# A two-group hybrid layer on one core: late weights split in small pieces along the convolution stage, the second weight part used last, query and key columns set between others

## The chip, the cores and the metric

The kernel runs on one core of a Trainium2 chip. The metric is device time in microseconds, the median of three runs of the whole kernel. TensorE (PE in the profile) multiplies, VectorE (DVE), ScalarE (ACT) and GpSimd (POOL) do the elementwise work, and all DMA transfers are issued by SyncE (SP), whose queue works in order.

## What is computed

One trunk layer for 2048 latent tokens and 256 context tokens, 1024 channels wide:

```python
h = rmsnorm(x) * norm_g * (1 + scale) + shift
q, k, v, g_att, a_conv, g_conv, x_pool, g_pool, x_ssm, g_ssm, g_mrg = split(h @ w_in)   # 70 x 128 columns
o_att  = windowed attention with a sink; latent queries and keys rotated, they also see the context keys
o_conv = silu(layernorm(depthwise_conv31(a0 * sigmoid(a1))))
o_pool = (mean over windows 2, 4, 8, 16 - x_pool) @ w_pool * scale
o_ssm  = z0 * sigmoid(z1),  z = gelu(bidirectional_scan(x_ssm)) @ glu_w
proj   = [o_n * silu(g_n)] @ w_br[n]                    # four branches
y = rmsnorm(x + gate * (sum_n(sigmoid(g_mrg[n]) * proj[n]) @ w_out)) * final_g
```

Everything is float32. The kernel keeps this accuracy on TensorE by splitting each operand into a high part, rounded to the matrix format, and a low part, the rest; a product is then three matmuls: high by high, low activation by high weight, high activation by low weight.

## The kernel before, in words

The 2304 tokens are cut into six chunks of 384 columns, two chunks to a group, three groups (0, 1, 2); channels lie on partitions. Tiles `hh` and `hl` hold the two parts of a group's normalized input, 8 slices of 128 channels each. A *dense column* is 128 columns of `w_in` for one group: `dense` (line 588) calls `mm3` (414) for both chunks, 24 matmuls of 128x128 by 128x384 each, so 48 per column. Before, `mm3` walks over the 8 slices and does the three products of a slice after one another.

A weight tile is split when it is first used (`split`, 357: `hi` is an ACT copy, `lo` a DVE subtraction, names `wis`, `wih`, `wil`) and both parts are stored to DRAM; for later groups `fetch` (390) loads them. `weights` (397) asks for them two columns ahead.

The order of TensorE's work is written out by hand, with a planner. `flow` (202) runs one dense stream and a list of background streams; each is a generator that yields what it needs next. A small cost model (`Clock`, 41) says when that will be ready; the first background stream that is ready goes, otherwise the dense stream makes a step (half a slice pair or the like; 10 steps to a column). `self.steps` counts dense steps, and some background work is paced by it (`METER`). PE then executes exactly this order and waits wherever the real data are later than the model said. The other engines' orders are made by the framework's scheduler.

Stages: (0) modulation, normalized inputs and the state-space branch's projections (`xssm`, 604); (1) all 66 columns of group 2 and then some of group 1, with the state-space scan in the background; (2) the rest of group 1, group 0's value, query and key columns, then its other columns and the 32 merge columns of group 1 again; in the background the depthwise convolution (`conv_taps`, DVE, ACT and POOL; `conv_norm`), the pools (`pool_tile`) and, from the 1350th microsecond on, attention; (3) per group the gated linear unit (`glu_group`), the four branch projections (`merge_group`, name `pj`) and the output projection (`out_group`), with `last_norm` in the background.

Names in the profile: `mm` is the PSUM tile of dense columns, `mge` the merge gates' copies out of it, `qf` and `qs` a query or key column and its swapped halves, `plh` and `plp` a pool's split and its product, `lnh` and `mean` the same for the convolution's layer norm, `dg` and `rb` the diagonal and the broadcast of a norm, `gy` the inputs of the linear unit, `wps`, `wph`, `wpl` the pieces of the late weights (`glu_w`, `w_br`, `w_out`) in `presplit` (374), and `wd_...` split weights in DRAM. Before, `presplit` is called from `gates_late` (1811) during the last 28 merge columns of stage 2, after attention has ended, up to three weights to a column. All instructions carry line 162, the recording helper, so they are told apart by their tiles.

Of the kernel before, what the change touches and what calls it, by code (L numbers as in the profile page):

```python
# [21 lines left out]
CH = 384  # L22
# [165 lines left out]
class K:  # L188
    def __init__(self, tc, A, outs):
        self.tc, self.A, self.O = tc, A, outs  # L190
        self.clock = Clock()
        self.nc = ClockedCore(self.clock, tc.nc)
        self.wplan, self.wgot, self.wsplit, self.waits, self.half, self.norms = [], {}, {}, {}, {}, 0
        self.wcache, self.have, self.steps = {}, {}, 0
# [179 lines left out]
    def presplit(self, key, ap):  # L374

        kt = self.WSRC[key[0]][1]
        src = self.A[self.WSRC[key[0]][0]][key[1:] if len(key) > 2 else key[1]]
        d = self.dp.tile([2, 128, kt, 128], F32, name="wd_" + "_".join(str(x) for x in key))
        for k in range(0, kt, 4):
            st = ap.tile([128, 4, 128], F32, name="wps", tag="p", bufs=2)  # L380
            self.load(st, src[:, k:k + 4])
            h = ap.tile([128, 4, 128], F32R, name="wph", tag="ph", bufs=3)
            l = ap.tile([128, 4, 128], F32R, name="wpl", tag="pl", bufs=3)
            self.hi(h, st)
            self.lo(l, st, h)
            for i, x in enumerate((h, l)):
                self.store(d[i][:, k:k + 4], f32(x))
        self.wcache[key] = d
# [25 lines left out]
    def mm3(self, outs, w, xs, kt):  # L414

        nc = self.nc
        wh, wl = w
        for c, o in enumerate(outs):
            yield (wh, wl, o, *xs[c](0), *xs[c](min(1, kt - 1)))
            for k in range(kt):  # L420
                for p, (wt, part) in enumerate(((wh, 0), (wh, 1), (wl, 0))):
                    nc.tensor.matmul(o, wt[:, k, :], xs[c](k)[part], start=(k == 0 and p == 0),
                                     stop=(k == kt - 1 and p == 2))
                if k % 2 == 1 and k + 2 < kt:
                    yield (*xs[c](k + 1), *xs[c](k + 2))
                elif k % 2 == 1:
                    yield ()
# [158 lines left out]
    PAIRS = {5: 0, 36: 37, 68: 69}  # L586

    def dense(self, ct, hs):
        xs = [lambda k, h=h: (h[0][:, k, :], h[1][:, k, :]) for h in hs]
        if ct in self.half:  # L590
            w, ps = self.half.pop(ct)
        else:
            w, ps = self.weights(("in", ct)), []
        for c in range(len(ps), len(hs)):
            ps.append(self.pm())
            yield from self.mm3([ps[c]], w, [xs[c]], 8)
            if c == 0 and ct in self.PAIRS and self.PB["mm"] > 2:
                nt = self.PAIRS[ct]
                self.half[nt] = self.weights(("in", nt)), [self.pm()]
                yield from self.mm3(self.half[nt][1], self.half[nt][0], xs[:1], 8)  # L600
# [32 lines left out]
    def col_qk(self, g, j, hs):  # L633
# [11 lines left out]
        qf = self.evq.tile([128, GT], F32, name="qf", tag="ev", bufs=3)  # L645
# [4 lines left out]
        qs = self.evq.tile([128, GT], F32, name="qs", tag="ev", bufs=3)  # L650
# [5 lines left out]
        r = self.evq.tile([128, GT], F32, name="qr", tag="ev", bufs=3)  # L656
# [3 lines left out]
        h = self.evq.tile([128, GT], F32R, name="qh", tag="evr", bufs=2)  # L660
        l = self.evq.tile([128, GT], F32R, name="ql", tag="evr", bufs=2)
# [6 lines left out]
        self.store(dst[1, j], f32(l))  # L668

    def col_v(self, g, hs):  # L670
        nc = self.nc
        ps = yield from self.dense(5, hs)
        vf = self.evq.tile([128, GT], F32, name="vf", tag="ev", bufs=3)
# [6 lines left out]
    def v_tokens(self, g, vf):  # L680

        nc = self.nc
        h = self.evq.tile([128, GT], F32R, name="vh", tag="evr", bufs=2)
        l = self.evq.tile([128, GT], F32R, name="vl", tag="evr", bufs=2)

        def half(a):
            tp = self.px("vtp", "x")[:, :CH]
# [67 lines left out]
    def conv_setup(self, cp):  # L755
# [11 lines left out]
        self.pw = cp.tile([128, 4, 128], F32, name="pw")  # L767
        self.load(self.pw, A["pool_w"])
        self.pwh = cp.tile([128, 4, 128], F32R, name="pwh")
        self.pwl = cp.tile([128, 4, 128], F32R, name="pwl")  # L770
        self.hi(self.pwh, self.pw)
        self.lo(self.pwl, self.pw, self.pwh)
# [5 lines left out]
    def convolution(self, chunks, mp):  # L778
# [14 lines left out]
        def pools():  # L793
            for gc in chunks:
                yield (lambda gc=gc: self.there("px", gc, 8),)
                for i in range(4):
                    yield from self.pool_tile(gc, i, mp)
# [18 lines left out]
    def conv_taps(self, gc, mp, taps):  # L816
# [4 lines left out]
        def tap(i, t):  # L821
            if t == 0:
                bufs[i] = mp.tile([128, CH + 60], F32, name="cbuf", tag="cbuf", bufs=3)
                self.n0 = self.seg_load(bufs[i], self.cx_d[i], gc, 15, self.CP) - 30
                accs[i] = mp.tile([128, self.W], F32, name="acc", tag="acc", bufs=8)
# [14 lines left out]
        for k in range(31):  # L840
# [5 lines left out]
            yield accs[i], lambda n=taps[0]: self.steps >= n * self.METER  # L846
        return accs

    def conv_norm(self, gc, accs, mp):
# [3 lines left out]
        for i in range(4):  # L853
# [5 lines left out]
            yield h, l, mean  # L859
            nc.tensor.matmul(mean, self.o512, h[:, :N], start=(i == 0), stop=False)  # L860
# [26 lines left out]
    def pool_tile(self, gc, i, mp):  # L887
# [735 lines left out]
    def last_norm(self, g, y, S, mp, chunks):  # L1623
# [5 lines left out]
        yield S, st  # L1629
        Sf = S.rearrange("p c t -> p (c t)")  # L1630
        for i in range(n):
# [7 lines left out]
        for m, c in enumerate(chunks):  # L1639
# [4 lines left out]
            yield dg, rb  # L1644
            nc.tensor.matmul(rb[:, :CH], self.ones, dg.rearrange("p i q -> p (i q)"), start=True, stop=True)
# [7 lines left out]
    def run(self, upto=9):  # L1653
        tc, nc, A = self.tc, self.nc, self.A
        ctx = ExitStack()
        with ctx:
# [28 lines left out]
            with era:  # L1685
# [11 lines left out]
                def qkv(g):  # L1697
                    return [([5], lambda h: self.col_v(g, h))] + [([j], lambda h, j=j: self.col_qk(g, j, h))
                                                                  for j in range(5)]
# [255 lines left out]
```

## Time and profile before

| | us |
|---|---|
| median of three runs | 3170.85 (3159.23 to 3172.75) |
| profiled execution, its own time | 3164.44 |
| its span | 3162.5 |
| PE busy | 2949.8 |
| DVE busy | 2031.0 |
| ACT busy | 1035.6 |
| POOL busy | 872.3 |

Mean granted clock of TensorE: 0.968 of full speed. DMA moved 711.13 MB, 225 GB/s over the span. An engine's busy time is the time in which at least one of its instructions ran; what stands in square brackets behind an instruction is the idle time just before it and what ended it.

### The profile page before, as it was taken

To read this page: it belongs to the slowest core of one execution; us is meant where nothing else is said; L and a number is where in the kernel's file an instruction comes from. 1 tells how busy PE (TensorE), PEld (TensorE's weight loads), DVE (VectorE), ACT (ScalarE), POOL (GpSimd) and SP (SyncE) were. 2 spreads that over 40 slices of the span, in tenths; PEclk is the share of its full clock that TensorE was granted. 3 is DMA by queue.
4 is the path that set the end of the run, shared out by engine and by line. 5 is a ranking of instruction groups with operands and counts; after the bars stand their busy time and mean duration, and the time that the engine had idled before them with its cause. 6 is when DMAs were issued, how large, how long until landed. Compare 5 with 4: busy or idle time off the path is not lost.

```text
span 3162.5 us, 45875 instructions
## 1 busy us (share of the span) xinstructions
PE 2949.8 (93%) x16316; PEld 2820.6 (89%) x16316; DVE 2031.0 (64%) x3468; ACT 1035.6 (33%) x1972; POOL 872.3 (28%) x1124
## 2 busy tenths in 40 slices
PE   8988999999989997899999999998867999999998
PEld 4888999998889987899999999998867999999897
DVE  6837887676776585779887687675313553653663
ACT  4523343333222342245554454443322011011010
POOL 0955434242442233323442222221000001001001
PEclk9999999999999998999999999999988999999998
DMA  9666555556655655665555554658998976976966
GB/s 359 205 226 218 203 208 200 209 193 220 239 180 176 219 185 201 223 183 181 174 173 172 161 164 144 226 160 290 326 347 286 327 228 228 342 245 224 320 195 233
DMA packets 355564, 711.13 MB, mean 225 GB/s; under 512 B 80808, under 2 KB 161288, under 8 KB 354056
## 3 DMA queue, kind: packets, MB, share of 16 engines
q1 hardware_dynamic: 355336, 708.21, 66.9%
q8 instruction: 128, 2.10, 0.3%
q14 instruction: 100, 0.82, 0.1%
HBM read 470.43 MB, written 229.83 MB: 221 GB/s over the span
## 4 chain that ended last, share of the span: by engine, by line
PE 51%; DMA 8%; DVE 4%; issue 1%; ACT 1%; SPq 1%; POOL 1%; DVEq 0%; ACTq 0%; POOLq 0%
PE mm L162 32%; PE pj L162 11%; PE ov L162 3%; PE sT L162 2%; DVE acc L162 2%; DMA pbuf<-px_d 1%; DMA wps<-w_br 1%; SPq L162 1%; DMA wps<-w_out 1%; DMA wbh<-wd_br 1%; PE mw L162 1%; PE mx L162 0%; DMA hh<-h_d 0%; POOL pls L162 0%; DMA wps<-glu_w 0%
## 5 line engine op out<-in xcount | busy, mean ns | idle before, releaser
L162 PE MATMUL mm<-hh,wih 128*128 128x384 f32 x3840 | 1310.3, 341 | 83.6 <-ACT mge L162 47.5
L162 PE MATMUL mm<-hh,wil 128*128 128x384 f32 x3840 | 1303.6, 339 | 33.5 <-DVE wil L162 32.6
L162 PE MATMUL mm<-hl,wih 128*128 128x384 f32 x3840 | 1301.2, 339 | 6.7 <-DMA hl<-h_d 6.6
L162 PEld LDWEIGHTS mm<-hh,wih 128*128 128x128 f32 x3840 | 733.0, 191 | 106.9 <-ACT mge L162 50.8
L162 PEld LDWEIGHTS mm<-hh,wil 128*128 128x128 f32 x3840 | 731.7, 191 | 39.8 <-DVE wil L162 38.5
L162 PEld LDWEIGHTS mm<-hl,wih 128*128 128x128 f32 x3840 | 732.6, 191 | 13.6 <-DMA hl<-h_d 9.5
L162 DVE SCALAR_TENSOR_TENSOR acc<-cbuf,cw,acc 128x384 f32<-128x384 f32 (+1 forms) x540 | 425.5, 789 | 9.0
L162 POOL TENSOR_TENSOR acc<-acc,cprod 128x384 f32<-128x384 f32 (+1 forms) x180 | 216.8, 1204 | 332.0 <-ACT cprod L162 318.5
L162 PE MATMUL pj<-hh,wbh 128*128 128x384 f32 x768 | 262.0, 341 | 3.2 <-DMA wbh<-wd_br 3.0
L162 PE MATMUL pj<-hh,wbl 128*128 128x384 f32 x768 | 260.2, 339 | 1.3 <-DMA wbl<-wd_br 1.3
L162 PE MATMUL pj<-hl,wbh 128*128 128x384 f32 x768 | 259.6, 338 | 0.0
L162 DVE TENSOR_TENSOR wil<-wis,wih 128x1024 fp32r<-128x1024 f32 x68 | 90.0, 1323 | 107.1 <-PE mm L162 56.0
L162 ACT ACTIVATE mge<-mm 128x384 f32<-128x384 f32 x192 | 92.9, 487 | 196.9 <-PE mm L162 193.4
L162 POOL TENSOR_TENSOR oS<-oS,osq 128x384 f32<-128x384 f32 x36 | 38.6, 1073 | 417.0 <-ACT osq L162 417.0
L162 PEld LDWEIGHTS pj<-hh,wbh 128*128 128x128 f32 x768 | 145.8, 190 | 5.2 <-issue 4.5
L162 PEld LDWEIGHTS pj<-hh,wbl 128*128 128x128 f32 x768 | 145.6, 190 | 3.2 <-DMA wbl<-wd_br 3.2
L162 PEld LDWEIGHTS pj<-hl,wbh 128*128 128x128 f32 x768 | 145.8, 190 | 0.9 <-issue 0.6
L162 DVE TENSOR_TENSOR pl<-p,ph 128x512 fp32r<-128x512 f32 x164 | 124.7, 766 | 33.1 <-ACT ph L162 32.8
L162 ACT ACTIVATE wih<-wis 128x1024 fp32r<-128x1024 f32 x68 | 72.0, 1060 | 191.8 <-DMA wis<-w_in 79.3
L162 DVE TENSOR_TENSOR wpl<-wps,wph 128x512 fp32r<-128x512 f32 x56 | 39.8, 713 | 145.5 <-ACT wph L162 142.2
L162 POOL TENSOR_TENSOR bo<-bo,br 128x768 f32<-128x768 f32 x12 | 22.1, 1842 | 384.0 <-DMA wih<-wd_out 217.0
L162 ACT ACTIVATE hh<-bo 128x768 fp32r<-128x768 f32 x48 | 38.8, 841 | 267.9 <-PE pj L162 166.4
(416 smaller groups left out, 4271.8 us busy)
## 6 DMA issues: line engine op xcount, KB each, us to landing
wih<-wd_in SPq DMA_DIRECT2D x132, 512.0 KB
wil<-wd_in SPq DMA_DIRECT2D x132, 512.0 KB
mg_d<-mge SPq DMA_DIRECT2D x96, 384.0 KB
mt<-mg_d SPq DMA_DIRECT2D x96, 384.0 KB
wis<-w_in SPq DMA_DIRECT2D x70, 512.0 KB
wd_in<-wih SPq DMA_DIRECT2D x66, 512.0 KB
wd_in<-wil SPq DMA_DIRECT2D x66, 512.0 KB
wbh<-wd_br SPq DMA_DIRECT2D x96, 256.0 KB
```

The source lines that it names most:

```text
L162: r = f(*args, **kw)
```

## The change

- `presplits` takes the place of `presplit`: a background stream of stage 2 that takes the late weights in pieces of 2 slices (256 columns) instead of 4, one piece each 0.9 * total / 112 dense steps, loads two pieces ahead.
- `mm3` does all high-by-high products of a chunk first, then all with the low activation part, then all with the low weight part; only the first columns on a newly made or loaded input (`fresh`) keep the order slice by slice.
- `cols` orders a group's columns as value, then pool and query columns in turn, a convolution column, the key column, the other convolution columns; three convolution columns of group 0 move behind the start of attention's setup. The first value column's chunk is paired with a pool column (`PAIRS`). Rings of the query work get 4 and 2 buffers (later 6 and 4) instead of 3 and 2.
- The pools are paced over the stage, and the matmuls of `conv_norm`, `pool_tile` and `last_norm` (groups 0 and 1) are put 3 or 4 us after their data by the planner's clock; they use other PSUM tags. `last_norm` waits for its own half of the sum only.
- The convolution's accumulators get 6 buffers instead of 8.

The core of the diff:

```diff
+    def presplits(self, keys, pool):
+        parts = [(key, k) for key in keys for k in range(0, self.WSRC[key[0]][1], 2)]
+        rate = 0.9 * self.total / len(parts)
+        got, to = [], {}
+        def fetch(key, k):
+            x = pool.tile([128, 2, 128], F32, name="wps", tag="wps", bufs=3)
+            src = self.A[self.WSRC[key[0]][0]][key[1:] if len(key) > 2 else key[1]]
+            self.load(x, src[:, k:k + 2])
+            got.append(x)
+        for p in parts[:2]:
+            fetch(*p)
+        for n, (key, k) in enumerate(parts):
+            yield (lambda n=n: self.steps >= n * rate,)
+            if n + 2 < len(parts):
+                fetch(*parts[n + 2])
...
+            h = pool.tile([128, 2, 128], F32R, name="wph", tag="wph", bufs=1)
+            l = pool.tile([128, 2, 128], F32R, name="wpl", tag="wpl", bufs=1)
+            self.hi(h, x)
+            self.lo(l, x, h)
             for i, x in enumerate((h, l)):
-                self.store(d[i][:, k:k + 4], f32(x))
+                self.store(to[key][i][:, k:k + 2], f32(x))
...
-    def mm3(self, outs, w, xs, kt):
+    def mm3(self, outs, w, xs, kt, fresh=False):
+        passes = ((0, 0), (0, 1), (1, 0))
+        seq = [(k, *p) for k in range(kt) for p in passes] if fresh else [(k, *p) for p in passes for k in range(kt)]
         for c, o in enumerate(outs):
...
+                nc.tensor.matmul(o, w[i][:, k, :], xs[c](k)[part], start=(n == 0), stop=(n == len(seq) - 1))
...
-    PAIRS = {5: 0, 36: 37, 68: 69}
+    PAIRS = {5: 22, 36: 37, 68: 69}
...
+        fresh = self.latest != hs[0][0].name
+        self.latest = hs[0][0].name
...
             for gc in chunks:
-                yield (lambda gc=gc: self.there("px", gc, 8),)
                 for i in range(4):
+                    yield (lambda gc=gc: self.there("px", gc, 8),
+                           lambda m=m: self.steps >= m * 0.88 * self.total / 24)
...
             yield h, l, mean
+            yield (self.clock.t + 3.0,)
...
-        ps = self.px("plp", "x")[:, :n]
+        ps = self.px("plp", self.PL)[:, :n]
         yield dh, dl, ps
+        yield (self.clock.t + 4.0,)
...
-        yield S, st
         Sf = S.rearrange("p c t -> p (c t)")
+        yield Sf[:, c0 * 128:(c0 + n) * 128], st
...
             yield dg, rb
+            yield (self.clock.t + (4.0 if g < 2 else 0.0),)
...
+                def cols(g):
+                    qk = [([j], lambda h, j=j: self.col_qk(g, j, h)) for j in range(5)]
+                    p, c = pools(g), convs(g)
+                    return ([([5], lambda h: self.col_v(g, h))] + [x for y in zip(p, qk) for x in y] +
+                            [c[0], qk[4]] + c[1:])
...
-                    todo = plan(bind(2, 2, pools(2) + qkv(2) + convs(2) + gates(2) + merges(2)) +
-                                bind(1, 1, qkv(1) + pools(1) + convs(1) + gates(1)) + bind(0, 0, qkv(0)))
+                    todo = plan(bind(2, 2, cols(2) + gates(2) + merges(2)) + bind(1, 1, cols(1) + gates(1)) +
+                                bind(0, 0, cols(0)[:11]))
...
-                    work = bind(0, 0, convs(0) + pools(0) + gates(0) + merges(0))
+                    work = bind(0, 0, cols(0)[11:] + gates(0) + merges(0))
...
+                    bg = self.convolution((4, 5, 3, 2, 1, 0), mp) + [self.presplits(rest, mp)]
+                    self.EB, self.VT = (6, 4), "s"
```

## Rows read from the trace of the kernel before

**Rows 1.** The page, part 1: PE's busy time, its share, its instructions.
```profile
PE 2949.8 (93%) x16316; PEld 2820.6 (89%) x16316; DVE 2031.0 (64%) x3468; ACT 1035.6 (33%) x1972; POOL 872.3 (28%) x1124
```
**Rows 2.** Table of stretches: start:end, length, busy PE, PEld, DVE, ACT, POOL, PEclk, DMA, GB/s.
```profile
2150.00:2390.00 240.00, 177.62 (x1001) 174.70 (x999) 79.54 (x126) 65.62 (x120) 16.07 (x15) 0.88 0.93 328
...
1215.00:1350.00 135.00, 106.75 (x539) 99.64 (x538) 90.40 (x127) 37.52 (x72) 50.60 (x45) 0.89 0.68 219
1350.00:2150.00 800.00, 795.53 (x4341) 752.31 (x4340) 617.12 (x1120) 398.02 (x796) 241.61 (x234) 1.00 0.56 173
250.00:1010.00 760.00, 709.70 (x4041) 680.87 (x4041) 577.51 (x834) 250.11 (x485) 311.63 (x396) 0.97 0.59 205
```
**Rows 3.** Waits of PE, whole span: for whom, us in total, times, longest us.
```profile
PE mm L162 <- DVE wil L162: 32.6, 16, 7.3
...
PE mm L162 <- ACT qf L162: 16.0, 5, 9.6
...
PE plp L162 <- ACT plh L162: 10.1, 3, 4.1
```
**Rows 4.** Waits of PE from 2150 to 2400 us.
```profile
PE mm L162 <- ACT mge L162: 45.1, 4, 42.0
PE mean L162 <- ACT lnh L162: 17.6, 1, 17.6
```
**Rows 5.** ACT in order of time: start us, us, instruction, [idle before, what ended it].
```profile
2387.05 2.31 ACT L162 ACTIVATE hh<-gy 128x768 fp32r<-128x768 f32 x3 [2.95 <-DMA wd_out<-wpl]
2389.84 1.36 ACT L162 ACTIVATE mge<-mm 128x384 f32<-128x384 f32 x3 [0.49 <-DVE hl L162]
```
**Rows 6.** Waits of ACT from 2150 to 2400 us.
```profile
ACT wph L162 <- DMA wps<-w_br: 54.2, 23, 6.4
```
**Rows 7.** Groups of instructions: shapes, count, busy us, mean ns, idle before.
```profile
L162 DVE TENSOR_TENSOR wil<-wis,wih 128x1024 fp32r<-128x1024 f32 x68 | 90.0, 1323 | 107.1 <-PE mm L162 56.0 <-ACT wih L162 38.7 <-DMA wd_in<-wih 6.2
...
L162 ACT ACTIVATE wih<-wis 128x1024 fp32r<-128x1024 f32 x68 | 72.0, 1060 | 191.8 <-DMA wis<-w_in 79.3 <-DVE wil L162 78.3 <-issue 25.8
...
L162 DVE TENSOR_TENSOR wpl<-wps,wph 128x512 fp32r<-128x512 f32 x56 | 39.8, 713 | 145.5 <-ACT wph L162 142.2 <-DMA wd_br<-wph 3.1
...
L162 ACT ACTIVATE wph<-wps 128x512 fp32r<-128x512 f32 x56 | 35.3, 630 | 116.2 <-DMA wps<-w_br 54.2 <-DMA wps<-w_out 35.1 <-DMA wps<-glu_w 11.4
```
**Rows 8.** PE in order of time: three waits for the low weight part.
```profile
302.52 0.69 PE L162 MATMUL mm<-hh,wil 128*128 128x384 f32 x1 [7.30 <-DVE wil L162]
...
317.05 0.45 PE L162 MATMUL mm<-hh,wil 128*128 128x384 f32 x1 [3.13 <-DVE wil L162]
...
511.30 0.69 PE L162 MATMUL mm<-hh,wil 128*128 128x384 f32 x1 [5.17 <-DVE wil L162]
```
**Rows 9.** PE in order of time: a wait for a query eviction and the matmuls after it.
```profile
916.90 0.69 PE L162 MATMUL mm<-hh,wih 128*128 128x384 f32 x1 [9.55 <-ACT qf L162]
917.39 0.52 PE L162 MATMUL mm<-hl,wih 128*128 128x384 f32 x1
...
923.09 0.34 PE L162 MATMUL mm<-hl,wih 128*128 128x384 f32 x1
923.27 0.33 PE L162 MATMUL mm<-hh,wil 128*128 128x384 f32 x1
```
**Rows 10.** PE in order of time: broadcasts of the last norm, group 0 and the end.
```profile
2692.19 1.65 PE L162 MATMUL rb<-dg,ones 128*128 128x384 f32 x2 [3.99 <-DVE dg L162]
...
3153.61 1.65 PE L162 MATMUL rb<-dg,ones 128*128 128x384 f32 x2 [4.85 <-DVE merged L162]
```
**Rows 11.** DVE in order of time: the last norm's multiplications at the end.
```profile
3149.79 3.76 DVE L162 SCALAR_TENSOR_TENSOR merged<-merged,fg,rb 128x384 f32<-128x384 f32 x7
3155.30 4.29 DVE L162 SCALAR_TENSOR_TENSOR merged<-merged,fg,rb 128x384 f32<-128x384 f32 x8 [1.74 <-PE rb L162]
```
**Rows 12.** Waits of SP's queue, whole span.
```profile
SPq L162 <- ACT wph L162: 56.8, 41, 4.4
```
**Rows 13.** Table of stretches, columns as in rows 2.
```profile
2300.00:2350.00 50.00, 47.78 (x275) 47.14 (x273) 6.18 (x9) 9.89 (x18) 0.00 (x0) 1.00 1.00 361
```

More of the change, by code (lines that the diff above doesn't have):

```diff
@@ L412, in weights @@
         return w
-    def mm3(self, outs, w, xs, kt):
+    def mm3(self, outs, w, xs, kt, fresh=False):
         nc = self.nc
-        wh, wl = w
+        passes = ((0, 0), (0, 1), (1, 0))
+        seq = [(k, *p) for k in range(kt) for p in passes] if fresh else [(k, *p) for p in passes for k in range(kt)]
         for c, o in enumerate(outs):
[L419 to L427, printed above, removed]
+            for n, (k, i, part) in enumerate(seq):
+                if n % 6 == 0:
+                    need = seq[n:n + 6]
+                    yield (*([o] if n == 0 else []), *{j: w[j] for _, j, _ in need}.values(),
+                           *(xs[c](q)[p] for q, _, p in need))
+                nc.tensor.matmul(o, w[i][:, k, :], xs[c](k)[part], start=(n == 0), stop=(n == len(seq) - 1))
+            if kt > 1:
+                yield ()
     def consts(self, cp):
@@ L593, in dense @@
             w, ps = self.weights(("in", ct)), []
+        fresh = self.latest != hs[0][0].name
+        self.latest = hs[0][0].name
         for c in range(len(ps), len(hs)):
             ps.append(self.pm())
-            yield from self.mm3([ps[c]], w, [xs[c]], 8)
+            yield from self.mm3([ps[c]], w, [xs[c]], 8, fresh)
             if c == 0 and ct in self.PAIRS and self.PB["mm"] > 2:
@@ L599, in dense @@
                 self.half[nt] = self.weights(("in", nt)), [self.pm()]
-                yield from self.mm3(self.half[nt][1], self.half[nt][0], xs[:1], 8)
+                yield from self.mm3(self.half[nt][1], self.half[nt][0], xs[:1], 8, fresh)
         return ps
@@ L1761, in beside @@
                         def beside():
-                            while todo and (bg or self.half or todo[0][0][0] < 5):
+                            while todo and (bg or self.half or self.open):
                                 yield from todo.pop(0)[1]
@@ L1774, in run @@
                     self.conv_setup(mp)
-                    work = bind(0, 0, convs(0) + pools(0) + gates(0) + merges(0))
+                    work = bind(0, 0, cols(0)[11:] + gates(0) + merges(0))
                     late = bind("1 again", 1, merges(1))
-                    self.METER = 0.88 * 10 * sum(len(ks) for ks, _ in todo + work + late[:28]) / (6 * 31)
+                    self.total = 10 * sum(len(ks) for ks, _ in todo + work + late[:28])
                     self.steps = 0
-                    bg = self.convolution((4, 5, 3, 2, 1, 0), mp)
+                    rest = [("glu", j) for j in range(4)] + [("br", n, d) for n in self.BR for d in range(8)]
+                    rest += [("out", d) for d in range(8)]
+                    bg = self.convolution((4, 5, 3, 2, 1, 0), mp) + [self.presplits(rest, mp)]
+                    self.EB, self.VT = (6, 4), "s"
                     for x in bg:
@@ L1797, in run @@
                                 bg.remove(md)
+                    self.PL = "x"
                     cb = pool(e1, "cb")
@@ L1809, in run @@
                         bg[:0] = at
[L1811 to L1820 removed]
+                        self.flow(self.chain([x for _, x in work[2:] + late[:28]]), bg)
                         self.steps = math.inf
```

68 lines of the change are left out of this document (28 added, 40 removed).

## The prediction

> **What bounds the kernel now.** I read the page first, then the stretches, then the waits of PE, then PE's instructions in order of time around each wait, and last what ACT and SP did in the same microseconds. On the page PE is busy 93% of the span [rows 1], so PE sets the time and every idle microsecond of it is a candidate; the other engines matter only where PE waits for them. The 212.7 us between PE's busy time and the span are what can be won at most, with the slow restarts. The table of stretches says where they lie [rows 2]: the attention stretch (1350 to 2150) loses 4.5 of 800 us, the stretch of the state-space branch (250 to 1010) 50 of 760, the change from group 1 to group 0 (1215 to 1350) 28 of 135, and the stretch in which the late weights are split (2150 to 2390) 62 of 240, with DMA engines 93% busy. The waits of PE then give names and sizes [rows 3, 4].
>
> A second cost stands behind each long wait. After 9.55 us without work the matmuls start 0.32 us apart instead of 0.18: 18 intervals from 917.39 to 923.09 [rows 9]. That is the lower of the two clock levels (1.2 against 2.4 GHz), and 5.70 us for 18 matmuls against 3.1 us at the upper level makes 2.6 us per restart. I use 2.6 us as the upper price of a restart, nothing as the lower.
>
> **Part 1, the late weights.** Now 56 pieces of 4x128 columns are loaded, split and stored in the last 240 us of the second stage. Each takes a load, one ACT copy (630 ns), one DVE subtraction (713 ns) and two stores [rows 7]; with 256 KB each way that is 14.7 MB in and 29.4 MB out. On top of the merge columns' own traffic this fills the DMA engines (share 1.00, 361 GB/s) [rows 13]. The page's groups and the waits show the rest: ACT waits 54.2 us for the pieces of one weight alone [rows 6], and ACT works in order, so the copy that frees a PSUM bank for PE stands behind. PE loses 45.1 us to that copy and 17.6 us to a normalization's copy, 62.7 us together [rows 4]. The longest wait ends when ACT gets past the input copies of the next stage, which had waited for the last store of the split weights [rows 5]. The change takes all pieces out of this stretch. What remains there is two weight loads and one store per column, 1.4 MB in 48 matmuls of 0.18 us, about 160 GB/s, under half of what row 13 moves. So I count 62.7 us, and 4 us for two restarts (0 to 5.2). Next late are the same input copies waiting for memory of the stage before, which the trace doesn't show without the pieces: 0 to 8 us, I take 2. **Gain 65 us (55 to 68).**
>
> Where they go: 112 pieces of half the size, each a load and two stores on SP's queue (336 instead of 168), between the weight loads and the attention's loads. By the two sizes in rows 7 DVE takes 713 ns for 512 columns and 1323 for 1024, so 1.19 ns a column and about 408 ns for 256; ACT by the same step 415. That makes 46 us on DVE (40 before) and 46 on ACT (35 before), over some 1240 us (from 1010 on, nine tenths of the stage). In the attention stretch DVE is busy 77% and ACT 50% [rows 2], so there is room, and PE's 4.5 idle us there say that their queues hardly hold PE now. The cost is nothing if the cover holds, and 112 x 0.408 = 46 us if each subtraction delays a result for which PE waits. I take 8 us, nearer to the lower end because the stretch with attention already runs at that low idle time. DMA: 56% share at 173 GB/s, so some 309 GB/s for this mix; 44 MB more in 1240 us add 35 GB/s, 11 points. **Cost 8 us (0 to 46).**
>
> **Part 2, the second weight part last.** The first matmul that reads the low part moves from third to seventeenth of a column's first 24. That is 14 x 0.18 = 2.5 us more for DVE's subtraction. PE waits for it 16 times, 32.6 us [rows 3]; three of these are longer than 2.5 us, 7.30, 5.17 and 3.13 [rows 8], and keep 4.8 + 2.7 + 0.6 = 8.1 us. **Gain 24.5 us (18 to 27 with a restart).** Against it: where activations come slice by slice, the old order spent three matmuls on each slice while it waited for the next; the new one has 16 of 24 left when the last slice comes, 13 more, 2.3 us. The dense columns keep the old order on a fresh input, but the first stage's projections and the output stage don't. That is up to six times 2.3 us at the start and four at the outputs; PE's waits for fresh slices are not among the large ones of rows 3, so I take one of each. **Cost 4.6 us (0 to 23).** Both matmuls and weight loads stay as many, so nothing is won or lost in rate.
>
> **Part 3, query and key columns between others.** Each such column needs an eviction, four small copies through DMA, a rotation and a split in one ring of three buffers. PE waits 16.0 us for their evictions [rows 3], 9.55 of it at once [rows 9]. With a pool or convolution column between, a ring slot has 96 matmuls, 17 us, instead of 8.6, and there are four slots, later six. The wait at 917 exceeds 8.6 us by little, so most goes. With the restart 18.6 us are there. **Gain 15 us (5 to 18.6).** The state-space work starts one column later, which costs nothing since as many dense columns remain beside it.
>
> **Part 4, small waits in the background.** Pool tiles are spread over the stage, and their matmuls and the normalizations' are put 3 to 4 us later in PE's order. PE now waits 10.1 us for the pool's split [rows 3], with restarts up to 17.9. Part of that comes from loads that arrive late, which no fixed 4 us covers, so I take half: **9 us (0 to 18).** The last norm's broadcast waits 3.99 us [rows 10] in each of the first two groups, 13.2 us with restarts; the next group's 192 matmuls of the gated linear unit, 34 us, can go ahead of it. **Gain 9 us (4 to 13).** At the end, the first half's normalization can now run under the second half's output matmuls: today the second broadcast waits 4.85 us for the first half's eight multiplications [rows 10, 11]. Its own broadcast has no extra delay there, so I take **3 us (0 to 5).**
>
> **Sum.** 65 - 8 + 24.5 - 4.6 + 15 + 9 + 9 + 3 = 112.9 us. The profiled execution took 3164.4 us, 6.4 less than the median of the runs (3170.85), inside their spread. 3164.4 - 112.9 = 3051.5, so 3052 us.
>
> **The rivals.**
> DVE becomes the bound of the attention stretch: each small subtraction stands in front of something that PE needs. 46 instead of 8 us: 3090 us. For it: 77% busy, in bursts, as the long waits for DVE in the stage before show [rows 8]. Against: the piece is the shortest work in that queue.
>
> The release goes to another wait: half of the 45.1 us comes back as ACT waits for memory that the convolution still holds. 3052 + 22 = 3074 us. For it: ACT's wait there was for memory of the stage before [rows 5].
>
> The change doesn't do what it says: pieces are due by the planner's count of dense steps, and other streams go first; if they pile up at the end as now, part 1 gives nothing. 3052 + 65 - 8 = 3109 us.
>
> Slower: SP works in order, and each piece puts two stores on it that wait for ACT and DVE. SP now waits 56.8 us in 41 such waits, 1.39 us each [rows 12]. If weight loads behind them come late and PE waits as long for each of the 112 pieces, that is 156 us: 3052 - 8 + 156 = 3200 us. It decides from 1.2 us a piece on. Against: weights are asked for two columns, 17 us, ahead, and the attention stretch has its own small loads on this queue while PE idles 4.5 us.
>
> Also slower: small transfers fill the DMA engines. The stretch has 44% of 1240 us free, 546 us; 336 transfers must take over 1.6 us of all engines each, 81 GB/s, under a quarter of the 361 GB/s of rows 13. At 60 GB/s 44 MB need 733 us, 187 too many: 3239 us. Against: that stretch moves 309 GB/s per full share with pieces as small among its loads. The Trainium skill, DMA: Bandwidth & Descriptors, section Bandwidth, speaks against the split: batch transfers to 1 MiB, with 341 GB/s for 1 MB and 138 for 64 KB. By its lower figure, an estimate from that page, 44 MB would need 319 us, less than what is free, so even the rule leaves the sum as it is; what the trace has on smaller pieces is only the mixed rate.
>
> **How the numbers follow.** Forecast 0.58; DVE bound 0.17; another wait 0.10; not as said 0.07; SP blocked 0.05; DMA full 0.03. Range: all gains at their upper ends and no cost give 65 + 3 + 27 + 18.6 + 18 + 13 + 5 = 150, 3015 us; on the upper side it takes in the DVE rival and nearly the one without part 1: 3105 us. A measurement of this kernel tells about 0.5%, 16 us. All cases but the two slow ones are faster by more; parts of the upper tails of these cases end within 0.5%. Faster 0.90, same 0.04, slower 0.06.
>
> **What would show it.** In the changed kernel's profile the stretch before the merges should show PE over 98% busy, DMA near half, and no wait for the merge gate's copy over 2 us. Waits for DVE's low part should be few and under 5 us, the waits for query evictions under 5 us in all, the broadcasts of groups 0 and 1 without wait, and only eight multiplications after the last output matmul. The count of split pieces should be 112, spread from 1010 us on. The prediction is wrong if PE's idle time in the attention stretch grows beyond 50 us, if new waits for weight loads (DMA) or for DVE stand there, or if the start stretch grows by over 14 us.

## The result, and the profile after

The changed kernel takes 3131.9 us (3124.43 to 3132.41), the kernel before on the same chip 3169.97 us: ratio 0.988 with the interval 0.985 to 0.991. It is 38 us faster where 113 were forecast. The profiled execution took 3132.41 us, its span is 3130.7 us. All counts of matmuls below are turned into time at 0.18 us each, the distance at the upper clock level [rows 9].

The page, part 1, answers to rows 1: the number of PE's instructions is the same, and the engines' busy times hardly move.

```profile
PE 2957.9 (94%) x16316; PEld 2823.2 (90%) x16316; DVE 2020.9 (65%) x3525; ACT 1035.9 (33%) x2029; POOL 874.4 (28%) x1124
```

The table of stretches (start:end, length, busy PE, PEld, DVE, ACT, POOL, PEclk, DMA, GB/s) answers to rows 2.

```profile
2150.00:2390.00 240.00, 238.26 (x1342) 232.95 (x1341) 70.27 (x124) 68.82 (x132) 27.61 (x30) 1.00 0.59 184
1215.00:1350.00 135.00, 125.06 (x665) 121.88 (x666) 96.78 (x162) 43.20 (x90) 48.58 (x36) 0.94 0.87 279
1350.00:2150.00 800.00, 755.68 (x4010) 706.38 (x4010) 617.93 (x1146) 390.75 (x812) 248.43 (x242) 0.98 0.65 201
250.00:1010.00 760.00, 719.33 (x4099) 688.44 (x4098) 567.42 (x825) 251.34 (x482) 310.63 (x395) 0.98 0.60 206
```

The late stretch gave what was said: 341 matmuls more, 61 us, at full clock. The attention stretch gave most of it away: 331 matmuls fewer, 60 us, and PE's idle time there went from 4.5 to 44.3 us; the other 20 us are matmuls that take longer on the mean (0.188 us of busy time instead of 0.183, at a granted clock of 0.98 instead of 1.00). The other two gained 126 and 58 matmuls, part of it because the work stands at other times now.

PE's waits over the whole span answer to rows 3 and 4.

```profile
PE mm L162 <- ACT tg L162: 28.1, 12, 5.4
PE rb L162 <- DVE dg L162: 12.8, 3, 4.8
PE mm L162 <- ACT mge L162: 11.1, 11, 2.9
...
PE mT L162 <- DVE mf L162: 8.8, 5, 3.3
PE mm L162 <- DVE wil L162: 8.1, 4, 5.9
PE sT L162 <- ACT p L162: 8.0, 5, 3.6
```

The wait of 42 us for `mge` is gone, `wil` fell from 32.6 to 8.1. New are waits for the gate columns' copies (`tg`) and for attention's steps (`mf`, `p`). What ACT waits for in the attention stretch says why:

```profile
ACT wph L162 <- DMA wd_out<-wph: 44.5, 19, 8.2
ACT wph L162 <- DMA wd_br<-wph: 40.8, 16, 5.2
```

ACT stands 85 us before the copies of pieces, because the one buffer of their high part is still being stored, and `tg`, `p` and every copy out of PSUM stand behind. Where the pieces run shows in the table of stretches of `wpl` alone (length, busy DVE and count, PEclk, DMA, GB/s):

```profile
1000.00:1200.00 200.00, 11.18 (x23) 0.98 0.70 226
1200.00:1400.00 200.00, 16.83 (x29) 0.92 0.87 273
1400.00:1600.00 200.00, 14.63 (x27) 0.96 0.69 211
1600.00:1800.00 200.00, 16.35 (x33) 0.98 0.68 212
1800.00:2000.00 200.00, 0.00 (x0) 0.98 0.57 165
```

All 112 are done before 1800 us; the plan's pace, nine tenths of the stage from 1010 us on, would have put the last near 2250. Their order on ACT, DVE and SP is the framework's scheduler's, and it lifts work that has no tie; the convolution's taps are tied to the instruction before them, the pieces are not.

### The profile page after: what moved, and what is told of

Read it like the earlier page. It is cut to its first block, busy times and chain, and to the rows that moved or that the text cites. A ratio compares the mean times of both kernels' runs of the same rounds, so it can differ in the third digit from the quotient of the medians.

```text
span 3130.7 us, 46156 instructions
## 1 busy us (share of the span) xinstructions
PE 2957.9 (94%) x16316; PEld 2823.2 (90%) x16316; DVE 2020.9 (65%) x3525; ACT 1035.9 (33%) x2029; POOL 874.4 (28%) x1124
## 4 chain that ended last, share of the span: by engine, by line
PE 37%; DMA 7%; DVE 5%; issue 1%; ACT 1%; SPq 1%; DVEq 0%; ACTq 0%
PE mm L162 20%; PE pj L162 12%; PE ov L162 2%; DVE acc L162 2%; PE sT L162 1%; DMA bs<-sg_d 1%; DMA wbh<-wd_br 1%; DMA wd_out<-wpl 1%; DMA wd_out<-wph 1%; SPq L162 1%; DMA wil<-wd_out 1%; DMA bo<-o_d 0%; PE mw L162 0%; DVE wpl L162 0%; DVE pl L162 0%
## 5 line engine op out<-in xcount | busy, mean ns | idle before, releaser
L162 PE MATMUL mm<-hh,wih 128*128 128x384 f32 x3840 | 801.9, 343 | 67.8 <-ACT tg L162 28.1
L162 PE MATMUL mm<-hh,wil 128*128 128x384 f32 x3840 | 784.7, 338 | 8.1 <-DVE wil L162 8.1
L162 PE MATMUL mm<-hl,wih 128*128 128x384 f32 x3840 | 789.3, 339 | 1.2 <-DMA hl<-h_d 1.2
L162 PEld LDWEIGHTS mm<-hh,wih 128*128 128x128 f32 x3840 | 688.2, 192 | 89.5 <-ACT tg L162 32.1
L162 PEld LDWEIGHTS mm<-hh,wil 128*128 128x128 f32 x3840 | 683.5, 190 | 12.8 <-DVE wil L162 9.5
L162 PE MATMUL pj<-hh,wbh 128*128 128x384 f32 x768 | 167.6, 341 | 1.6 <-DMA wbh<-wd_br 1.6
L162 PE MATMUL pj<-hh,wbl 128*128 128x384 f32 x768 | 165.6, 338 | 0.0
L162 PE MATMUL pj<-hl,wbh 128*128 128x384 f32 x768 | 165.6, 338 | 0.0
L162 DVE TENSOR_TENSOR wpl<-wps,wph 128x256 fp32r<-128x256 f32 x112 | 59.0, 527 | 116.0 <-ACT wph L162 38.7
L162 DVE SCALAR_TENSOR_TENSOR mt<-mt,pj 128x384 f32<-128x384 f32 x144 | 79.4, 551 | 68.0 <-PE pj L162 62.4
```

What stands on the lines that cost most here:

```text
L162: r = f(*args, **kw)
```

## The experiments

Times are medians, ratios are to the kernel before. Diffs are against the changed kernel unless said otherwise.

**Where the pieces run.** Each piece is tied behind the last instruction on ACT and DVE, as the taps are (e1).

```diff
-            self.hi(h, x)
-            self.lo(l, x, h)
+            self.behind = dict(self.clock.last)
+            self.queue("scalar", self.nc.scalar.activation(h, x, AF.Copy))
+            self.queue("vector", self.nc.vector.tensor_tensor(l, x, f32(h), op=OP.subtract))
```

> The changed kernel, with each piece's ACT copy and DVE subtraction tied behind the instruction that was issued before it on its engine, as the convolution's taps are; nothing else. Theory A (the framework's scheduler moves the pieces ahead of their due step, all 112 are done by 1792 us, and with one buffer each ACT and DVE stand still until a store has landed): the pieces spread to about 2150 us, ACT's waits for wph on its own stores fall from 135 us to under 30, the stretch from 1400 to 2000 us holds again about 3200 matmuls instead of 3019, and the time falls by 25 to 40 us, to 3092 to 3107. Theory B (the work of 112 subtractions on a busy DVE is what delays the attention): the pieces only move, the time stays within 10 us of 3132.

3097.5 us, 0.979 (0.977 to 0.981): 29 us from the order alone by the ratios, 34 by the medians. 16 to 21 pieces now stand in each 200 us. In the runs' tables of the convolution stage and the late stretch, e1 first:

```profile
1000.00:2200.00 1200.00, 1143.11 (x6247) 1084.81 (x6246) 918.64 (x1634) 551.87 (x1156) 368.00 (x354) 0.99 0.69 217
2200.00:2400.00 200.00, 197.29 (x1127) 196.40 (x1126) 46.32 (x72) 36.46 (x66) 7.20 (x6) 0.99 0.74 249
```

The changed kernel has 6062 matmuls in the first of these stretches, 185 fewer, 33 us:

```profile
1000.00:2200.00 1200.00, 1127.81 (x6062) 1064.32 (x6061) 887.85 (x1616) 535.08 (x1122) 365.04 (x351) 0.97 0.68 213
```

The two below ran with the split work left out (e2: the stores take the unsplit piece) and with part 1 undone (e3: `gates_late` and `presplit` of before, parts 2 to 4 as changed).

> The changed kernel with the pieces loaded and stored twice as they are; the split itself, ACT's copy and DVE's subtraction, is left out (part of the computation). All DMA stays. Theory A and theory B: the attention stretch gets back what it lost, 3085 to 3100 us. Theory C (SP's queue or the DMA engines are what the pieces cost): the time stays within 10 us of 3132.

> The changed kernel with part 1 undone: the late weights are split again in the last 28 merge columns, in pieces of four slices; all other parts stay. If part 1's new place costs what the attention stretch lost (238 matmuls, some 43 us) and its old place what was read from the trace before (62.7 us): 3132 - 43 + 63 = 3152 us. If the other parts cost the attention stretch its time (pass order, pools and planner's delays), that stretch stays slow and the time is about 3132 + 63 = 3195 us.

e2: 3098.5 us, 0.979 (0.977 to 0.981), though its transfers are lifted too and fill 0.92 and 0.94 of the DMA engines in 1100 to 1300; in 1000 to 2200 it has 6253 matmuls, about as many as e1. e3: 3114.3 us, 0.984 (0.982 to 0.986). This is the most telling run: without part 1 the kernel is 13 us (ratios) to 18 us (medians) faster than with it. Its stretches:

```profile
1000.00:2200.00 1200.00, 1174.48 (x6495) 1122.49 (x6494) 889.53 (x1553) 534.71 (x1068) 372.81 (x362) 0.99 0.61 189
2200.00:2400.00 200.00, 148.74 (x842) 147.51 (x841) 57.45 (x79) 48.09 (x81) 1.85 (x1) 0.87 0.90 321
```

So the pieces cost 433 matmuls, 78 us, as the changed kernel has them, and 248, 45 us, when tied; the late stall that they replace is 285 matmuls, 51 us (only 37 of 56 old pieces still fit behind attention in e3, the rest are split at their first use). 78 - 51 = 27 more than e3 against 13 to 18 measured, 45 - 51 = 6 less against 17: the signs agree, and the sizes within some 10 to 14 us. Part of the late stall stands after 2400 us: over 2200 to 2600 e3 has 1958 matmuls, the changed kernel 2269 and e1 2277, 56 and 57 us, and the two differences become 22 more and 12 less.

**The order of the products** (e4: `fresh` always true, so the low weight part is needed third again).

> The changed kernel with the order of products undone alone: all columns slice by slice. Theory D (PE's wait for the low weight part only moved to the next thing that a busy DVE and ACT release late, the PSUM banks of the gate columns, tg): waits for wil come back, some 30 us in the stretch of the state-space branch, those for tg go, and the time is within 10 us of 3132. If the order gained what I forecast (24.5 us), it is 3150 to 3160.

3147.8 us, 0.9945 (0.993 to 0.996), 16 us (medians) to 20 us (ratios) slower; PE's waits for `wil` are back:

```profile
PE mm L162 <- DVE wil L162: 36.9, 20, 7.4
```

**The single buffers** (e5: `wph` with two buffers, not tied; e8: the same, tied; one buffer of attention's `es` pays for it).

> The changed kernel, pieces not tied, but two buffers instead of one for each piece's high part (paid by one buffer less in the attention's exponentials). Theory A (the cost of the pieces is mainly where they run, because the scheduler lifts all of them to 1100 to 1800 us): pieces stay early and the time stays above 3115 us, though ACT's waits for its own stores of wph fall by half or more. Theory B (the single buffer is what blocks ACT, wherever the pieces stand): 3095 to 3110 us, as with tied pieces, and the attention stretch 1400 to 2000 gets most of its 238 lost matmuls back.

> Tied pieces and two buffers for their high part. If ACT's waits for its own stores still cost PE time with tied pieces (waits for the gate column's eviction 17.5 us in all there), 3080 to 3092 us and those waits fall by half; if the cost that is left is not in these buffers, 3094 to 3101 us as with tied pieces alone.

3133.5 us, 0.989 (0.987 to 0.991), and 3095.9 us, 0.978 (0.975 to 0.980): nothing in either case. In e5 ACT's waits for its own stores fell from 135 us to 26, but its waits for DVE's `wpl`, which holds the buffer next, rose from 19.2 to 105.0, and DVE's for its own stores from 55 to 83. Most of the waiting moved, and a wait that moves is not a cost removed.

```profile
ACT wph L162 <- DVE wpl L162: 105.0, 48, 4.8
```

**Later, or with a lighter engine** (e6: tied, none before 28% of the stage; e12: tied, the subtraction on POOL).

```diff
-        rate = 0.9 * self.total / len(parts)
+        off = 0.28 * self.total
+        rate = (0.9 * self.total - off) / len(parts)
...
-            yield (lambda n=n: self.steps >= n * rate,)
+            yield (lambda n=n: self.steps >= off + n * rate,)
```

> Pieces tied to their place and none before 28% of the stage's dense steps (about 1400 us), so that the change from group 1 to group 0 with its reload of activations and the convolution's catching up is free of them; 13 instead of 9 pieces per 100 us afterwards. Theory A1 (what is left of the pieces' cost with tied pieces, some 38 us, stands mostly in 1100 to 1400): 1000 to 1400 us gets back to 2170 matmuls as in the run with late pieces (2043 with tied pieces from the start), 3072 to 3085 us. Theory A2 (the cost goes with the number of pieces, on DVE, ACT or DMA, wherever they are): the same count of matmuls is lost later in 1400 to 2200 and the time stays at 3092 to 3105 us.

> Tied pieces as in the first run (3097 us), with the subtraction on POOL, which is 30% busy in this stretch, instead of DVE, 77% busy. If DVE's queue is what the pieces hold up: 3070 to 3085 us, the waits of PE for DVE's mf and acc gone. If it is ACT or the transfers, 3094 to 3105 us. If POOL, slower at a subtraction, keeps ACT waiting for the buffer of the high part: over 3105 us.

e6: 3109.7 us, 0.982 (0.980 to 0.984), 12 us slower than e1. Against e1, 1200 to 1400 got 72 matmuls back and 1400 to 2200 lost 158. e12: 3099.0 us, 0.979 (0.977 to 0.981), as on DVE.

**Work or transfers** (both on e3's kernel, with an extra stream at the pieces' places; e9: 112 splits of one loaded tile without transfers; e10: the loads and stores without splits).

> The kernel with the late weights split late (third run, 3114 us) and beside it, from 1010 us on at the planned places, 112 extra pairs of an ACT copy and a DVE subtraction of 256 columns from one loaded tile, with no transfers and nothing that reads them. Only extra work, the late splits stay. Theory S (the cost of the pieces is their place in the queues of ACT and DVE): 35 to 45 us more, 3148 to 3160 us, with some 250 matmuls fewer in 1000 to 2200. Theory T (it is their transfers and the waits for these): 3114 to 3124 us.

> The same kernel with late splits, and beside it the 112 extra loads of 128 KB and two stores each to memory that nothing reads, the stores tied to their places in SP's order, with no ACT or DVE work. Theory T: 35 to 45 us more, 3148 to 3160 us, with some 250 matmuls fewer in 1000 to 2200 and waits for hh, qa and weights behind it. Theory S: 3114 to 3124 us. If both runs cost about half, the two add up, and if neither costs more than 10 us, it is the waits between them (ACT for the store, DVE for ACT) that cost.

e9: 3114.8 us, 0.984 (0.982 to 0.986), as without (3114.3). e10: 3188.3 us, 1.007 (1.005 to 1.009), 74 us more, twice what was expected. The first stretch of e9 and of e10, then what SP waits for in e10 from 1010 to 2200:

```profile
1000.00:2200.00 1200.00, 1172.43 (x6465) 1120.01 (x6464) 930.18 (x1656) 566.38 (x1177) 374.64 (x365) 0.99 0.60 188
```

```profile
1000.00:2200.00 1200.00, 1107.68 (x6005) 1051.79 (x6004) 843.62 (x1485) 494.21 (x995) 351.23 (x348) 0.97 0.67 211
```

```profile
SPq L162 <- DMA wx_br<-wps: 93.4, 55, 4.5
...
SPq L162 <- DMA wx_out<-wps: 38.7, 22, 3.6
...
SPq L162 <- DMA wx_glu<-wps: 25.5, 13, 4.7
```

DVE and ACT carry the splits for nothing. The transfers cost 490 matmuls, 88 us. SP stands 158 us before loads whose buffer is still being stored, with loads of weights and attention's tiles behind them. This is the price of that arrangement and not of the bytes: the whole pieces, tied, move as many and cost 45 us, and here 80 of the 112 were stored by 1650 us, ahead of the plan.

**Whose queue waits** (e13: tied, the high part's store on ACT's queue, the low part's split and store on POOL; e14: all 336 transfers on POOL's queue; e16: both parts in one tile, one store on SP).

> Pieces tied as before, the subtraction on POOL, and each store issued from the queue of the engine that made its data: the high part's on ACT's, the low part's on POOL's. SP keeps the loads alone. Same bytes, same number of transfers. If SP's order is the cause (theory Q): SP's 154 us of waits for wph and wpl are gone, 1000 to 2200 gets back to 6450 to 6500 matmuls, 3055 to 3068 us. If the load on the DMA engines is the cause (theory D): 3092 to 3103 us as with tied pieces. If ACT and POOL pay for the issuing of 224 stores themselves: over 3105 us, with new waits of PE for ACT.

> Tied pieces, subtraction on DVE, all 336 transfers of the pieces issued from POOL's queue. Under theory Q 3060 to 3080 us, the more so as POOL now stands in the stores' waits instead of SP, and what waits for POOL (the rotation, the third part of the convolution's sum) pays some of it. Under theory D 3092 to 3103 us.

> Tied pieces, both parts of a piece in one tile and stored by one transfer: 112 stores of 256 KB instead of 224 of 128 KB, all on SP. Bytes as before, SP waits once a piece instead of twice, but as long in all, since the wait for the high part was only the first half of it. Theory Q: about as with tied pieces, 3090 to 3100 us, or up to 10 us better by the waits for wph. Theory D in the form that the number of transfers counts: 3075 to 3088 us.

e13: 3109.6 us, 0.981 (0.979 to 0.984); it did not take SP out of the waits, since SP's loads now wait 104.6 us for POOL to free their tiles. e14: 3110.2 us, 0.982 (0.980 to 0.983). There SP does wait for pieces hardly any more (`wph` 10.2 us), and still:

```profile
1000.00:2200.00 1200.00, 1136.75 (x6190) 1078.89 (x6189) 943.96 (x1631) 543.92 (x1138) 528.48 (x685) 0.98 0.68 215
```

```profile
ACT wph L162 <- DMA wd_br<-wph: 32.3, 9, 7.9
ACT wph L162 <- DVE wpl L162: 27.2, 10, 5.0
```

So SP's order alone is not the cause; the same waits stand in ACT's and DVE's queues, and POOL's, which now issues the stores, stands 252 us before them until `wph` or `wpl` is ready. e16: 3089.9 us (3083.26 to 3096.27), 0.975 (0.973 to 0.978): half as many stores are worth 8 us by the medians, though its runs and e1's overlap.

**The waits out of all queues** (e17: as e16; loads one piece ahead, the store a whole piece after its split, two buffers, each step tied, on SP too).

```diff
-            self.store(to[key].rearrange("i p k c -> p i k c")[:, :, k:k + 2], f32(hl))
+            out.append((key, k, hl))
+            if len(out) > 1:
+                put(*out.pop(0))
...
+        def put(key, k, hl):
+            self.behind = dict(self.clock.last)
+            self.queue("sync", self.store(to[key].rearrange("i p k c -> p i k c")[:, :, k:k + 2], f32(hl)))
```

> As the run with one store, and every step of a piece is issued only when what it needs is a whole piece (about 11 us) old: load one piece ahead, split, and the store one piece after its split, each tied to its place in its queue, loads and stores too; both parts have two buffers. Same 44 MB, same 336 less 112 transfers. Theory W (the waits in the in-order queues cost, not the bytes): waits of SP, ACT and DVE for pieces under 20 us together, 1000 to 2200 back to 6400 to 6500 matmuls, 3055 to 3070 us. Theory D (the bytes on the DMA engines): waits gone and time as with one store, 3083 to 3096 us.

3076.2 us (3068.82 to 3080.09), 0.970 (0.967 to 0.973): the fastest version, 56 us below the changed kernel, with the same bytes. The run changes loads ahead, stores, buffers and ties together; apart from the one store (e16), no run parts them. SP's waits for pieces from 1010 to 2200, in e1 and then in e17, and e17's stretch:

```profile
SPq L162 <- DVE wpl L162: 104.8, 65, 5.3
...
SPq L162 <- ACT wph L162: 48.8, 36, 5.6
```

```profile
SPq L162 <- DVE wphl L162: 47.0, 39, 6.2
...
SPq L162 <- ACT wphl L162: 6.8, 13, 2.2
```

```profile
1000.00:2200.00 1200.00, 1163.44 (x6379) 1109.11 (x6378) 922.76 (x1649) 557.45 (x1163) 371.90 (x362) 0.98 0.70 220
```

Added over SP, ACT and DVE, the waits for pieces are 461 us in the changed kernel, 297 in e1 and 139 in e17; the loss of matmuls against e3 in 1000 to 2200 is 78, 45 and 21 us. The sum is no measure by itself: in e8 it is 200 us with a loss of 48, and without the splits 86 with 44 (e2) and 158 with 88 (e10).

**What is left** (e18: as e17, no piece between 12% and 27.5% of the stage, about 1180 to 1395 us).

> As e17, with no piece between about 1180 and 1395 us (12% to 27.5% of the stage's dense steps) and 10.2 instead of 9 per 100 us elsewhere. If the loss left is the meeting with the reload: 1200 to 1400 gets back to about 1050 matmuls, the other stretches stay, 3060 to 3068 us, the first clear gain over e17. If it goes with the number of pieces: the 70 matmuls are lost in 1400 to 2300 instead, 3072 to 3082 us.

3089.5 us, 0.977 (0.975 to 0.978), 13 us (medians) to 21 us (ratios) slower than e17. 1200 to 1400 went from 986 to 1016 matmuls, not to 1050, and the rest of the stage lost more than that. So the last 21 us are not won by keeping this place free. Whether the 139 us of waits that remain or the load on the DMA engines (share 0.70 against 0.61) make them is not settled. The same question stands for part of the changed kernel's 78 us: in e2 the bunched transfers alone, at shares of 0.92 and 0.94, go with a loss of 44.

**No early split at all** (e11: the stream taken out, so each late weight is split at its first use in the last stage; e15: the same, branch weights loaded three and split two columns ahead).

> No split of the late weights ahead at all: group 1's last part and group 2 and 0 read and split each late weight where it is first used, in the last stage, as the other weights are, and store it for the later groups. This takes 44 MB and 112 ACT copies and 112 DVE subtractions out of the convolution stage and puts 56 times 512 columns into the last stage, where DVE is half idle but the DMA engines are 80 to 87% busy. If the place is free there: 3114 less the late stalls of 51 us, with the restart, 3057 to 3065 us. If the last stage's loads and stores can't carry it (a third more bytes per column in the first group): its matmuls come late by 48 columns times 0.5 to 1 us, 3085 to 3110 us.

> No split ahead, as in the run with 3101.55 us, but a branch weight is loaded three columns and split two columns ahead instead of two and one. There PE waited 23.0 us for the high part of such weights, and 2200 to 2600 lost some 200 matmuls, 36 us. If the load's and split's lead time is what was short: those waits under 5 us and 3065 to 3080 us. If the DMA engines are full there (share 0.81 to 0.83 in these stretches): 3090 to 3102 us.

3101.6 us, 0.980 (0.978 to 0.982), and 3094.6 us, 0.977 (0.975 to 0.979). The convolution stage is as free as in e3 (6479 matmuls in e15), but 2200 to 2600 has 2082 matmuls against 2281 in e17. The place in the last stage costs 36 us and is no better.

**The last norm's gate** (e7: tied pieces; the first two merged columns of a group may go before the norm has ended).

```diff
                 if i == 0:
-                    yield (lambda: not self.norms,)
+                    if d >= 2:
+                        yield (lambda: not self.norms,)
```

> Tied pieces as in the first run, and the first two merged columns of a group no longer wait for the last norm before them (two of the ten buffers are free anyway). If the gate is what keeps the second broadcast of groups 0 and 1 uncovered, the two waits for dg of 4.85 us each before rb at about 2640 and 2890 us fall under 1 us, and with the restarts behind them the time falls by 9 to 14 us against tied pieces: 3084 to 3090 us. If the broadcast waits because DVE comes to it late (eight multiplications before it), the waits stay and the time stays at 3097 us.

3099.8 us, 0.978 (0.976 to 0.981), no gain against e1. From 2600 to 2950 PE's wait for `dg` fell from 9.7 to 5.7 us, and a new one came:

```profile
PE pj L162 <- DVE merged L162: 7.5, 2, 5.9
PE rb L162 <- DVE dg L162: 5.7, 2, 3.5
```

The branch columns now run ahead, and then wait for DVE, which must do the eight multiplications of each half before it empties their banks.

## Why the prediction was wrong, step by step

**Part 1, gain 65: right.** 2150 to 2390 went from 1001 to 1342 matmuls, and no wait over 2 us is left there. **Part 1, cost 8 (0 to 46): the step that failed.** It cost 78 us by the matmuls (e3 against the changed kernel; 64 to 74 us by the runs' times and the late stall), more than its upper end. Three things in it were wrong. First, "over some 1240 us": the pieces were taken to stand where the planner puts them, but only PE's order is written out; they ran in 700 us, and tying them gave back 29 to 34 us (e1). Second, the bound was made from DVE's busy time, 112 x 0.408 us. That work costs nothing (e9), although a subtraction took 0.527 us on the mean:

```profile
L162 DVE TENSOR_TENSOR wpl<-wps,wph 128x256 fp32r<-128x256 f32 x112 | 59.0, 527 | 116.0 <-ACT wph L162 38.7 <-DMA wd_br<-wpl 29.1 <-DMA wd_out<-wpl 15.2
```

Third, the three transfers of a piece were counted as bytes on the DMA engines, 11 points of share, which is near what came (0.61 in e3, 0.68 in the changed kernel, 0.70 in e17). With these bytes and shares the loss was 78, 45 and 21 us (changed kernel, e1, e17), so most of it goes with when each transfer is due. What the traces show there is the time to landing: with one buffer for each part, a queue that touches a piece stands until the transfer before is complete, and holds everything behind it. How the 78 us divide between these waits and the bunching of the transfers stays open. Part of the evidence was in the profile: SP's 1.39 us per store [rows 12] is the same wait, and the change doubles the number of stores. ACT's 54.2 us [rows 6] were waits for loads; in the changed kernel those are small, and ACT waits 135 us for its own stores (4 us before). The old `presplit` had three buffers for each part, the new stream has one; with two (e5) these waits are 26 us.

**The rivals.** The DVE bound falls by e9 and e12. SP blocked had the right mechanism for one of the queues (121 us of waits in the changed kernel and 154 in e1, where 156 were supposed), but in e1 PE lost less than a third as much, and SP is only one of the queues (e14). The pieces not where they were said to be: yes, but early instead of late. DMA engines full of small transfers: not over the stage, where the share is 0.68; in the bunch of e2 they come near it. In e14 POOL's queue moved 42.95 MB in 10.6% of 1190 us of all engines, 126 us, so some 340 GB/s:

```profile
q0 software_dynamic: 15718, 42.95, 10.6%
```

The Trainium skill, DMA: Bandwidth & Descriptors, section Bandwidth, has 138 GB/s at 64 KB and 341 at 1 MB; for pieces of 128 KB this run is at the upper figure. From issue to landing the same transfers took 3.3 to 4.9 us in the median. The Trainium skill, DMA: Bandwidth & Descriptors, section Anatomy of one DMA, has about 2 us plus the bytes at 436 GB/s for a transfer from this queue, which makes an estimate of 2.3 us for 128 KB. The trace shows 1.4 to 2.1 times that beside this kernel's other traffic, and agrees that the bytes are the smaller part: at 340 GB/s they take 0.4 us.

**Part 2, 24.5 less 4.6: right.** Waits for `wil` fell by 24.5 us, the start (0 to 250 us) has 4.8 us more idle time, and undoing the order costs 16 to 20 us (e4) where 19.9 were counted. Part of the wait went on to the banks of the gate columns: `tg` was 1.0 us before and is 28.1 now.

**Part 3, 15: right in size.** The wait for `qf` fell from 16.0 to 1.1 us, and 750 to 1000 gained 80 matmuls, 14 us; other parts act there as well.

**Part 4, pools 9: right in kind,** the waits for `plp` are gone; what that gave by itself no run shows. **The broadcasts, 9: wrong.** Two waits of 3.99 us became two of 4.85. Here are PE and DVE in group 0 of the kernel before, then DVE and PE of the changed kernel:

```profile
2685.31 0.81 PE L162 MATMUL rb<-dg,ones 128*128 128x384 f32 x2
```

```profile
2687.39 4.28 DVE L162 SCALAR_TENSOR_TENSOR merged<-merged,fg,rb 128x384 f32<-128x384 f32 x8
2691.59 0.55 DVE L162 TENSOR_TENSOR dg<-ident,rs_i 128x384 f32<-128x384 f32 x1
```

```profile
2662.14 4.29 DVE L162 SCALAR_TENSOR_TENSOR merged<-merged,fg,rb 128x384 f32<-128x384 f32 x8
2666.34 0.55 DVE L162 TENSOR_TENSOR dg<-ident,rs_i 128x384 f32<-128x384 f32 x1
```

```profile
2661.29 0.81 PE L162 MATMUL rb<-dg,ones 128*128 128x384 f32 x2
2666.95 1.01 PE L162 MATMUL rb<-dg,ones 128*128 128x384 f32 x1 [4.85 <-DVE dg L162]
```

The first broadcast had no wait before either. The second half's diagonal stands behind the first half's eight multiplications in both kernels; in the changed one the dense stream has reached its gate by then (e7). The step named 34 us of cover and did not look at what stands between the two broadcasts on DVE. **The tail, 3: right,** at the upper end of its range. One round of eight multiplications stands after the last output matmul (it ends at 3115.1) instead of two [rows 11]; from there to the last multiplication it is 12 us, 17 before:

```profile
3121.11 1.62 PE L162 MATMUL rb<-dg,ones 128*128 128x384 f32 x2 [3.10 <-DVE dg L162]
```

```profile
3108.81 4.29 DVE L162 SCALAR_TENSOR_TENSOR merged<-merged,fg,rb 128x384 f32<-128x384 f32 x8 [1.99 <-PE rb L162]
...
3122.77 4.29 DVE L162 SCALAR_TENSOR_TENSOR merged<-merged,fg,rb 128x384 f32<-128x384 f32 x8 [1.80 <-PE rb L162]
```

Together, parts 2 to 4 were to give 55.9 us, and e3, which has them and late splits (though with 37 of the 56 pieces), is 50 us faster than the kernel before. Part 1 was to give 65 - 8 = 57 us; against e3 it took 13 to 18. Nearly all of the 75 us by which the forecast missed lie there.

**The signs.** Of those that were to show it, the stretch before the merges, the waits for `wil` and for query evictions and the tail came out, except that one wait for `wil` reached 5.9 us; the spread of the pieces and the broadcasts of groups 0 and 1 did not. PE's idle time in the attention stretch stayed under 50 us (44.3) and the start under 14 (4.8). The sign that did come was new waits for DVE in the attention stretch, 24 us where 2.5 stood before.

## What to carry to other kernels

Work that is moved into a busy stretch is priced by its waits, not by its busy time: for each queue that it passes, ask what it stands on and whether that is a whole step old when its turn comes. Give it buffers, put the store one step after its data, and tie it to its place on every engine whose order a scheduler makes. A wait that is taken off one queue by a buffer or another queue often shows up on the next, so look at all queues before and after. The sum is a pointer, not a price: with the second buffer on tied pieces it fell from 297 to 200 us (e1, e8), and the time stayed. The time of a run decides.

## What the runs showed of the hardware

Issuing the 336 transfers from POOL's queue cost POOL 334 instructions more and 163 us of busy time (365 to 528 us in 1000 to 2200, changed kernel and e14), some 0.49 us each by this trace, in which spans on POOL are rough. The subtraction of 256 columns took 0.506 us on the mean on DVE in e9 (0.418 in the median) and 0.949 us on POOL in e12:

```profile
L162 DVE TENSOR_TENSOR wpl<-wps,wph 128x256 fp32r<-128x256 f32 x112 | 56.7, 506 | 16.6 <-ACT wph L162 16.5
```

```profile
L162 POOL TENSOR_TENSOR wpl<-wps,wph 128x256 fp32r<-128x256 f32 x112 | 106.2, 949 | 160.9 <-ACT wph L162 86.9 <-DMA wd_br<-wpl 19.8 <-DMA o_d<-ob 13.2
```
